# MoE block on one core: the order of the experts ends with each group's smallest one, and most output rows are summed and stored during the last weight loads

## The chip, the cores and the metric

The kernel runs on one core of a Trainium2 chip. The metric is the device time of one execution in microseconds (us), lower is better; three runs of the kernel before took 1245.50, 1245.51 and 1246.52 us, median 1245.51 us.

## The reference

One layer: a layer norm, a token mixer (gMLP and gated DeltaNet), a second layer norm `h1`, a hierarchical mixture of experts, a third layer norm. There are 512 tokens of width 1024. Only the mixture and the last norm matter here:

```python
grp = argmax(softmax(xt @ w_rg + b_rg))           # one of 4 groups for each token
le = (xt @ w_re + b_re)[token, grp]               # 8 experts in that group
top_v, top_i = lax.top_k(le, 2)                   # the token's two experts
gate = p_grp * softmax(top_v)
y_e = (silu(x @ w1[e]) * (x @ w3[e])) @ w2[e]     # for each of its two experts
out = layer_norm(alpha * h1 + gate_1 * y_1 + gate_2 * y_2, ln2_g, ln2_b)
```

All 32 experts are stored; an expert that gets no token need not be computed. Both experts of a token lie in the same group. Routing the reference's own inputs gives these numbers of tokens, expert 0 first, a row for each group: 1 0 2 2 1 2 1 1; 57 55 40 18 94 83 37 130; 34 22 82 104 15 18 126 19; 0 11 8 5 26 15 13 2. Two experts (1 and 24) are empty. No expert has over 160 tokens.

## The kernel before, in words

Up to about 700 us the mixer, `h1` and the router run. The router (`Router`) turns the choice of each token into `ord`, the order in which experts are worked on, and into lists of token indices for each place in that order. `Router.order` (L1088) sees only the first 256 tokens, since it has to be ready before the rest are routed.

The experts are then streamed (`Experts.run`, L1313). A "block" b is a place in the order, 0 to 31. Each block has six weight loads of 1 MB: chunks 0 to 3 are w1 and w3, chunks 4 and 5 are w2. SyncE (SP) issues them (`load_big`, L391) into a ring of 18 buffers (`raws`), in the order (b, 0 to 3), (b-1, 4), (b-1, 5). A load waits until the tensor engine (PE) has read what lay in its buffer, and until the load eight back has landed, because there are eight semaphores for SP's and ScalarE's transfers. From block 3 on a block without tokens skips its loads.

In iteration b the PE does `up` for block b (L1440), transposes the next block's tokens (`turn_x`, L1407), does `down` for block b-1 (L1467) and transposes the hidden values of block b (`turn`, L1457). ScalarE (ACT) and VectorE (DVE) form silu and product in `gate` (L1450). A block of n tokens is done in a small part of 32 rows and up to two large parts of 64, whichever its count needs (`units`, L1247). At the end of an iteration `store_y` (L1478) copies the outputs of block b-1 out of PSUM and GpSimd (POOL) issues five conditional stores to `y_dram`. POOL also gathers the tokens of block b+2 (`fetch`).

In the order before, experts go round the groups, the ones that look empty are put together ahead of the last four, and the last four are simply the last non-empty ones. For these inputs the blocks 24 and 25 are empty and the last four blocks have 126, 13, 130 and 19 tokens.

After the last block comes everything else: `finish_rows` (L1004) loads h1 (four tiles of 128 tokens by 1024) and the rows of the norms' gains and biases, 4.2 MB, and forms alpha * (h1 * g + b). A loop over blocks of overflowing experts (L1661) runs zero times here, but all engines meet there with all their transfers done. `finish` (L1022) gathers eight tiles of 128 rows of `y_dram` (L1028), adds them with their gates to the four tiles (L1034), takes the statistics (L362 to L374), normalizes (ACT, L1037), applies gain and bias (L1038, L1039) and stores the four tiles (L1040).

Of the kernel before, what the change touches and what calls it, by code (L numbers as in the profile page):

```python
# [1043 lines left out]
class Router:  # L1044
# [43 lines left out]
    def order(self):  # L1088
# [9 lines left out]
        v.tensor_scalar(f.rearrange("p (j g) -> p j g", g=4), self.cps[:, NT].rearrange("p (g j) -> p j g", g=4),
                        0.0, None, op0=OP.is_gt)
        v.memset(f[:, 0:NPRE], 1.0)  # L1100
        r = W.tile([128, E], F32, name="or_")
        v.tensor_tensor_scan(r, cst["ones"][:, 0:E], f, 0.0, OP.mult, OP.add)
# [7 lines left out]
        v.scalar_tensor_tensor(out=p1, in0=r, scalar=-1.0, in1=p1, op0=OP.add, op1=OP.add)  # L1110
        v.tensor_tensor(out=p1, in0=p1, in1=p0, op=OP.subtract)
        v.tensor_tensor(out=p1, in0=p1, in1=f, op=OP.mult)
        v.tensor_tensor(out=p0, in0=p0, in1=p1, op=OP.add)
        eq = W.tile([128, E, E], F32, name="oeq")
# [621 lines left out]
```

## Time and profile before

| what | us |
|---|---|
| median of three runs | 1245.51 |
| the profiled execution: its own time | 1246.53 |
| its span, first to last instruction | 1244.8 |
| last matmul ends | 1187.3 |
| eight gathers start | 1200.2 |
| last DVE instruction ends | 1239.1 |

Busy in the span: PE 1039.3 us, DVE 646.2, ACT 403.1, POOL 193.5. The table of 40 slices is read like this: each digit is the busy share of 31.1 us in tenths. The transfers are at 9 in nearly all slices from the 24th to the 37th, and in the last three, after the last weights, no engine and no queue is at 9.

In the timeline rows the first number is the start in us, the second the duration; "x4" is the number of instructions merged in the row; in brackets stand the engine's idle time before it and what ended that. In rows of windows the columns are: stretch, its length, busy time (and count) of PE, its weight loads, DVE, ACT, POOL, the granted PE clock, the busy share of the 16 DMA engines, GB/s.

### The profile page before, as it was taken

The numbers are of one execution on the slowest core, as the hardware profiler recorded it, in microseconds if no ns is written. First come the engines' busy times: TensorE is split into PE (matmuls) and PEld (weight loads), VectorE is DVE, ScalarE is ACT, GpSimd is POOL, SyncE is SP. The second block draws the span as 40 slices with busy tenths as digits, with TensorE's granted clock in tenths as the row PEclk, the third lists the DMA queues.
The fourth block names the chain that finished last, engine by engine and source line by source line (L and its number), as shares of the span: only waits on it lengthen the run. The fifth ranks groups of instructions, "written<-read, shape, count | busy, mean of one in ns | idle before, by whom it ended". The sixth has DMA issues, their size and how long they took to land. (4 is left out here: it accounts for less than half of the span.)

```text
span 1244.8 us, 19415 instructions
## 1 busy us (share of the span) xinstructions
PE 1039.3 (83%) x6880; PEld 687.0 (55%) x6880; DVE 646.2 (52%) x1356; ACT 403.1 (32%) x844; POOL 193.5 (16%) x377
## 2 busy tenths in 40 slices
PE   4999999999999999999999588787877586579810
PEld 2888788867777777667887333443333242234300
DVE  7566444567667777754865444533223232433246
ACT  6333355444555455435431311111111111211111
POOL 1000100212212132200001101111111101111043
PEclk9999999999999999999999698997979897799965
DMA  5422533899221121114672799999999999999832
GB/s 172 153 84 69 160 95 110 284 341 362 70 68 58 45 68 52 34 52 152 238 308 91 295 385 409 391 411 400 414 390 415 399 414 399 377 387 387 349 115 111
DMA packets 76899, 296.10 MB, mean 238 GB/s; under 512 B 9328, under 2 KB 34176, under 8 KB 53216
## 3 DMA queue, kind: packets, MB, share of 16 engines
q1 hardware_dynamic: 66672, 272.13, 58.0%
q0 software_dynamic: 7504, 17.20, 4.3%
q10 hardware_dynamic: 2592, 4.99, 1.2%
q8 instruction: 87, 1.43, 0.5%
q14 instruction: 44, 0.36, 0.1%
HBM read 277.36 MB, written 50.35 MB: 263 GB/s over the span
## 5 line engine op out<-in xcount | busy, mean ns | idle before, releaser
L214 PE MATMUL psi<-hTh,lo 128*128 128x512 f32 x448 | 183.0, 410 | 1.6 <-DVE lo L214 1.6
L214 PE MATMUL psi<-hTh,hi 128*128 128x512 f32 x448 | 183.5, 413 | 0.9 <-ACT hi L214 0.5
L214 PE MATMUL psi<-hTl,hi 128*128 128x512 f32 x448 | 183.1, 411 | 0.0
L1455 DVE TENSOR_TENSOR h<-h,u 128x640 f32<-128x640 f32 x32 | 26.3, 822 | 279.2 <-ACT h L1454 267.2
L214 DVE TENSOR_TENSOR lo<-raw,hi 128x1024 fp32r<-128x1024 f32 x74 | 91.3, 1234 | 79.6 <-ACT hi L214 78.9
L1447 PE MATMUL u<-raw,xs 128*32 128x256 f32 x1472 | 102.1, 426 | 29.8 <-DMA raw<-in_w 28.2
L214 ACT CAST hi<-raw 128x1024 fp32r<-128x1024 f32 x74 | 77.5, 1047 | 117.3 <-PE psi L214 100.2
L1447 PE MATMUL u<-raw,x 128*64 128x512 f32 x448 | 103.6, 618 | 5.9 <-PEq L1387 2.9
L214 PEld LDWEIGHTS psi<-hTh,lo 128*128 128x128 f32 x448 | 84.4, 188 | 21.3 <-issue 3.9
L214 PEld LDWEIGHTS psi<-hTh,hi 128*128 128x128 f32 x448 | 84.6, 189 | 20.3 <-issue 2.8
L214 PEld LDWEIGHTS psi<-hTl,hi 128*128 128x128 f32 x448 | 84.4, 189 | 17.2 <-issue 1.6
L1447 PEld LDWEIGHTS u<-raw,xs 128*32 128x32 f32 x1472 | 50.9, 120 | 73.4 <-DMA raw<-in_w 38.6
L1454 ACT ACTIVATE h<-u 128x640 f32<-128x640 f32 x32 | 22.6, 705 | 204.5 <-PEq L1389 160.9
L1447 PEld LDWEIGHTS u<-raw,x 128*64 128x64 f32 x448 | 35.5, 143 | 68.6 <-issue 60.0
L1475 PE MATMUL y<-raw,hT 128*64 128x512 f32 x224 | 60.1, 672 | 11.5 <-PEq L1387 9.2
L1475 PE MATMUL yz<-raw,hT 128*32 128x256 f32 x736 | 55.2, 437 | 16.4 <-PEq L1427 5.9
L1464 ACT COPY hT<-t 128x128 f32<-128x128 f32 x32 | 8.5, 266 | 184.0 <-PE t L1461 172.7
L1483 DVE COPY ysmall<-yz 32x256 f32<-32x256 f32 x128 | 53.3, 417 | 16.8 <-PE yz L1475 15.3
L214 DVE SCALAR_TENSOR_TENSOR acc<-xp,cols,acc 128x512 f32<-128x512 f32 x72 | 54.7, 760 | 4.7 <-ACT acc L214 3.5
L1492 POOL DMA_DIRECT2D y_dram<-ylarge x128 | 19.5, 155 | 194.1 <-DMA y_dram<-ysmall 114.8
L1475 PEld LDWEIGHTS yz<-raw,hT 128*32 128x32 f32 x736 | 26.3, 121 | 35.7 <-issue 18.0
L1422 PE MATMUL t<-ident,mh 64*128 64x64 f32 x256 | 23.5, 237 | 25.8 <-PEq L1389 20.0
(437 smaller groups left out, 1864.9 us busy)
## 6 DMA issues: line engine op xcount, KB each, us to landing
raw<-in_w SPq DMA_DIRECT2D x192, 1024.0 KB
raw<-in_wt SPq DMA_DIRECT2D x73, 512.0 KB
y_dram<-zero SPq DMA_DIRECT2D x48, 512.0 KB
y_dram<-ylarge POOLq DMA_DIRECT2D x128, 128.0 KB
raw<-in_wv SPq DMA_DIRECT2D x8, 512.0 KB
raw<-in_wo SPq DMA_DIRECT2D x4, 1024.0 KB
y_dram<-ysmall POOLq DMA_DIRECT2D x32, 128.0 KB
vt<-in_x SPq DMA_DIRECT2D x4, 512.0 KB
```

The lines of the kernel that those rows point to most:

```text
L214: op._ins = getattr(getattr(self.nc, op.attr), op.name)(*map(real, op.args), **{k: real(x) for k, x in op.kw.items()})
L1422: nc.tensor.transpose(self.t[0][:, k * NA:k * NA + NA], r[0][:, k * 128:k * 128 + 128], ident[0:NA, 0:NA])
L1447: self.nc.tensor.matmul(self.u[q * r:(q + 1) * r, NP if p is None else p, 0:c], x[:, k, r0:r0 + r], self.raw[b, k // 2][:, o:o + c], start ...
L1454: self.nc.scalar.activation(out=h, in_=u[:, :, 0], func=AF.Silu)
L1455: self.nc.vector.tensor_mul(out=h, in0=h, in1=u[:, :, 1])
L1464: self.nc.scalar.copy(out=x[:, n], in_=self.t[1][:, 0:128])
L1475: self.nc.tensor.matmul(y[q * r:(q + 1) * r, 0:c], t[:, i, j * r:(j + 1) * r], self.raw[b, 4 + k // 2][:, o:o + c], start=k == 0, stop=k == 3)
L1483: nc.vector.tensor_copy(out=small[:, q], in_=self.y0[q * 32:(q + 1) * 32, 0:256])
L1492: nc.gpsimd.dma_start(out=dst[:, q * 512:(q + 1) * 512], in_=large[q * 64:(q + 1) * 64, p], cond=n > 32 + 64 * p)
```

## The change

It has five parts.

1. **Order of the experts.** The groups still take turns, but each expert that looks empty is moved back by 10.5 places among the others, and the expert of each group with the fewest (at least one) of the first 256 tokens goes to the last four places. For these inputs the empty experts stand at blocks 10 and 12 (and two experts that only look empty, with 1 and 2 tokens, at 26 and 27), the blocks 22 and 24 have 126 and 130 tokens, and the last six blocks 1, 2, 2, 18, 5 and 15. Since both experts of a token are of one group, a token is in the last four blocks at most once.
2. **Loads.** From block RT = 26 on, the chunks of block b go into the buffers of block b-2. The six buffers of block 23 are thereby free for other use, and the ring is 12 buffers deep from then on. The last two chunks of block 25 are loaded ahead of the first four of block 26.
3. **The other rows.** A new class `Tail` is called at the head and the end of each iteration from 26 on. It loads the rows of gains and biases and h1 (iteration 26, now issued by ACT), gathers for the tokens' rows outside the last four blocks (29 and 30; rows of the last four blocks point to a row of zeros), adds, normalizes and stores all four tiles (30 and 31).
4. **The late rows.** The tokens of the last four blocks, up to 32 each, have a tile `F` of their own: 4 x 32 rows with their h1, their gates and their other expert's output. The outputs of the last four blocks stay in a buffer `Y` and are not stored to `y_dram`. The last block's part is added from PSUM, then comes the norm of `F`, and a scatter writes its rows over the ones stored before; it waits for the four stores.
5. **The branch.** `flag` is zero if each of the last four blocks has at most 32 tokens, no two non-empty ones are of a group, and nothing overflows. If it isn't, the whole of the old finish runs after all, ahead of the last step. For these inputs (2, 18, 5 and 15 tokens, four groups) it is zero.

The diff, cut to its core:

```diff
@@ Router.order
+        f = W.tile([128, E], F32, name="of_")
+        v.tensor_scalar(f, self.cps[:, NT], 0.0, None, op0=OP.is_gt)
+        v.scalar_tensor_tensor(out=sc, in0=self.cps[:, NT], scalar=32.0, in1=cst["jx"], op0=OP.mult, op1=OP.add)
...
+        v.tensor_reduce(out=mn, in_=gj(sc), axis=AX.X, op=OP.min)
+        v.tensor_tensor(out=gj(lt), in0=gj(sc), in1=bc(mn, 8, 2), op=OP.is_equal)
...
+        v.scalar_tensor_tensor(out=f, in0=f, scalar=-10.5, in1=cst["seq"], op0=OP.mult, op1=OP.add)
+        v.scalar_tensor_tensor(out=f, in0=lt, scalar=128.0, in1=f, op0=OP.mult, op1=OP.add)
+        eq = W.tile([128, E, E], BF, name="oeq")
+        v.tensor_tensor(out=eq, in0=bc(f, E, 1), in1=bc(f, E, 2), op=OP.is_lt)
+        v.tensor_reduce(out=pos, in_=eq, axis=AX.X, op=OP.add)
+        v.tensor_tensor(out=eq, in0=bc(pos, E, 1), in1=bc(cst["iota"][:, 0:E], E, 2), op=OP.is_equal)
@@ Experts.run
+            if tail and b == RT:
+                steps = steps[:-6] + steps[-2:] + steps[-6:-2]
-                self.raw[b, c] = kk.load_big(blk[1]()[c], conds.get(b))
+                self.raw[b, c] = kk.load_big(blk[1]()[c], conds.get(b), self.raw[b - 2, c] if b >= RT else None)
...
+            if tail and b >= RT:
+                tail(b, 0)
             if b < nb:
                 self.parts(b, self.up)
-                load(4)
+                if not tail or b not in (RT - 3, E - 2):
+                    load(4)
@@ class Tail, __call__
+        if (b, at) == (RT, 0):
...
+            self.load_rows(R_L1G, R_L1B)
+            for x in (self.g2, self.b2):
+                act.activation(out=x, in_=x, func=AF.Copy, scale=ALPHA)
+            for t in range(NT):
+                act.dma_start(out=self.f[t], in_=self.h1_dram[t * 128:(t + 1) * 128, :])
...
+        elif (b, at) == (RT + 3, 0):
+            self.take(0, 1)
+        elif (b, at) == (RT + 4, 0):
+            self.add(0, 1)
+            self.take(2, 3)
+            self.gather(self.O, self.y_dram, r.lrow, NYROW)
+        elif (b, at) == (RT + 4, 1):
+            self.apply((0, 1), self.stats(0, 1))
+        elif (b, at) == (RT + 5, 0):
+            self.add(2, 3)
+            v.scalar_tensor_tensor(out=self.F, in0=self.O, scalar=r.lgate[:, 1:2], in1=self.F, op0=OP.mult, op1=OP.add)
+            self.m = self.stats(2, 3)
+        elif (b, at) == (RT + 5, 1):
+            self.apply((2, 3), self.m)
...
+        elif (b, at) == (E, 2):
+            for q in range(4):
+                f = F[128 - 32:128, q * 256:(q + 1) * 256]
+                v.scalar_tensor_tensor(out=f, in0=ex.y0[q * 32:(q + 1) * 32, 0:256], scalar=r.lgate[128 - 32:128, 0:1], in1=f,
+                                       op0=OP.mult, op1=OP.add)
...
+            x = g.indirect_dma_start(out=kk.a["out"], out_offset=bass.IndirectOffsetOnAxis(ap=r.lidx, axis=0), in_=F,
+                                     in_offset=None, bounds_check=T - 1, oob_is_err=False)
@@ build
-    kk.finish_rows(h1_dram)
...
+    flag = nc.values_load(r.flag[0:1, 0:1], min_val=0, max_val=64, skip_runtime_bounds_check_because="sums of counts")
+    with tc.If(flag > 0):
...
+        kk.finish_rows(h1_dram)
...
+        kk.finish(RS, r, y_dram)
+        nc.vector.tensor_scalar(r.lidx, r.ordl, 0.0, float(T), op0=OP.mult, op1=OP.add)
+    with tc.manual_schedule():
+        tail(E, 2)
```

What is left out: `Router.rest` forms the late rows' indices, gates, `flag` and the gather's indices with some 30 small DVE instructions spread over the first iterations, and a 12 KB table in memory; a second constant `jx`.

On SP, the end of its queue before (in_w2 is w2 of the last two blocks; the h1 and row loads of `finish_rows` follow):

```order
L399 DMA raw9_5390<-in_w2 128x2048
L399 ISA
L399 DMA raw10_5391<-in_w2 128x2048
L1387 UNCONDITIONAL_BRANCH
L1389 UNCONDITIONAL_BRANCH
L399 ISA
L399 DMA raw11_5392<-in_w2 128x2048
L1013 DMA raw12_5393<-h1_dram_57 128x1024 x2
L1387 UNCONDITIONAL_BRANCH
L1389 UNCONDITIONAL_BRANCH
L1013 DMA raw13_5394<-h1_dram_57 128x1024 x2
L1015 DMA raw14_5395<-in_rows 128x1024 x2
```

And with the change, the same place:

```order
L402 DMA raw9_5396<-in_w2 128x2048
L402 ISA
L402 DMA raw14_5401<-in_w2 128x2048
L1456 UNCONDITIONAL_BRANCH
L1458 UNCONDITIONAL_BRANCH
L402 ISA
L402 DMA raw15_5402<-in_w2 128x2048
L1456 UNCONDITIONAL_BRANCH
L1458 UNCONDITIONAL_BRANCH
L1688 DMA out<-raw11_5398 128x1024 x2
L1857 TENSOR_LOAD flag_5442
L1858 COMPARE_AND_BRANCH
```

The h1 and row loads have left SP's queue; two of the four output stores stand behind the last weight load, and then comes the branch on `flag`.

On POOL, the gathers of `y_dram` before (`yi` holds the row of each token's output; the stores are those of the last block, the branch is the loop over overflowing blocks):

```order
L1492 DMA y_dram_59<-ylarge_11918 64x512
L1661 REGISTER_ALU
L1661 COMPARE_AND_BRANCH
L1661 UNCONDITIONAL_BRANCH
L1028 DMA raw16_5397<-y_dram_59,yi_5429 128x1024 x2
L1028 DMA raw17_5398<-y_dram_59,yi_5429 128x1024 x2
L1028 DMA raw4_4806<-y_dram_59,yi_5429 128x1024 x2
L1028 DMA raw5_4807<-y_dram_59,yi_5429 128x1024 x2
```

With the change, iteration 30 on POOL (`yie` are the rows with the late ones replaced, `lrow` the other rows of the late tokens, `mh` the buffer O):

```order
L1658 DMA raw12_5399<-y_dram_59,yie_5436 128x1024 x2
L1658 DMA raw13_5400<-y_dram_59,yie_5436 128x1024 x2
L1456 UNCONDITIONAL_BRANCH
L1458 UNCONDITIONAL_BRANCH
L1658 DMA mh_4466<-y_dram_59,lrow_5441 128x1024
L1496 UNCONDITIONAL_BRANCH
L1500 UNCONDITIONAL_BRANCH
L1456 UNCONDITIONAL_BRANCH
L1458 UNCONDITIONAL_BRANCH
L1567 ISA
L1567 DMA y_dram_59<-ylarge_11554 64x512
```

The gathers now stand between iterations of the expert loop, ahead of the conditional stores of a block that has no large part, and no longer behind the loop's branch.

On DVE, from the product in `gate` of the last block (`h`) to the branch, before (the copies take the two last blocks out of PSUM; L1019 and L1020 form h1 * g + b):

```order
L1455 TENSOR_TENSOR h_11532<-h_11532,u_5407 128x640
L1387 UNCONDITIONAL_BRANCH
L1389 UNCONDITIONAL_BRANCH
L1483 COPY ysmall_11578<-yz_5406 32x256 x4
L1387 UNCONDITIONAL_BRANCH
L1389 UNCONDITIONAL_BRANCH
L1483 COPY ysmall_11632<-yz_5406 32x256 x4
L1019 TENSOR_TENSOR raw12_5393<-raw12_5393,raw14_5395 128x1024 x2
L1020 TENSOR_TENSOR raw12_5393<-raw12_5393,raw14_5395 128x1024
L1659 TENSOR_LOAD nov_5426
L1661 COMPARE_AND_BRANCH
```

And with the change (the copies go to `Y`, L1685 and L1687 are gain and bias of tiles 2 and 3, the 96x1024 instruction adds the first three late blocks to `F`):

```order
L1524 TENSOR_TENSOR h_11692<-h_11692,u_5413 128x640
L1456 UNCONDITIONAL_BRANCH
L1458 UNCONDITIONAL_BRANCH
L1557 COPY raw7_4812<-yz_5412 32x256 x4
L1685 TENSOR_TENSOR raw11_5398<-raw11_5398,raw6_4811 128x1024 x2
L1456 UNCONDITIONAL_BRANCH
L1458 UNCONDITIONAL_BRANCH
L1687 TENSOR_TENSOR raw11_5398<-raw11_5398,raw6_4811 128x1024
L1629 SCALAR_TENSOR_TENSOR raw7_4812<-raw7_4812,lgate_5440 96x1024
L1857 TENSOR_LOAD flag_5442
L1858 COMPARE_AND_BRANCH
```

Tiles 2 and 3 get their gain and bias between the last block's `gate` and the branch, on the same queue; the last block's copies are gone from there.

More of the change, by code (lines that the diff above doesn't have):

```diff
@@ L1039, in finish, with behind @@
             (nc.gpsimd if t < 3 else v).tensor_tensor(out=f, in0=f, in1=self.l2b, op=OP.add)
-            nc.sync.dma_start(out=a["out"][t * 128:(t + 1) * 128, :], in_=f)
+            self.behind(nc.sync.dma_start(out=a["out"][t * 128:(t + 1) * 128, :], in_=f), self.stores)
+    def behind(self, x, others):
+        for y in others:
+            self.tc.add_manual_dep(x.ins, y.ins.name, mybir.DependencyInfo(
+                mybir.DependencyClass.Sync, mybir.DependencyReason.DATA), reason="rows of the output")
 class Router:
@@ L1096, in order @@
                 nc.tensor.matmul(self.cps[:, NT], cst["ones_bf"], q[:, k], start=t + k == 0, stop=t + k == 2)
+        gj = lambda x: x.rearrange("p (g j) -> p g j", g=4)
         f = W.tile([128, E], F32, name="of_")
[L1098 to L1102, printed above, removed]
@@ L1110, in order @@
[L1110 to L1114, printed above, removed]
-        v.tensor_tensor(out=eq, in0=bc(p0, E, 1), in1=bc(cst["iota"][:, 0:E], E, 2), op=OP.is_equal)
-        g.tensor_tensor(out=eq, in0=eq, in1=bc(cst["seq"], E, 1), op=OP.mult)
+        v.tensor_scalar(f, self.cps[:, NT], 0.0, None, op0=OP.is_gt)
@@ L1194, in rest @@
         v.tensor_copy(out=self.nov, in_=inc[:, NX * E - 1:])
+        v.tensor_tensor(out=fs[:, 0:1], in0=fs[:, 0:1], in1=inc[:, NX * E - 1:], op=OP.add)
+        v.tensor_copy(out=self.flag, in_=fs[:, 0:1])
         exc = R.tile([128, NX, E], F32, name="exc")
@@ L1311, in clear, with run @@
                                       func=AF.Copy, scale=0.0)
-    def run(self, blocks, more=None, clear=None):
+    def run(self, blocks, more=None, clear=None, tail=None):
         nc, kk, nb = self.nc, self.kk, len(blocks)
@@ L1367, in run @@
                 self.parts(b - 1, self.down)
-                load(2)
+                if not tail or b != RT - 2:
+                    load(2)
             next(more, None)
@@ L1371, in run @@
                 self.turn(b)
-            if b:
-                self.store_y(b - 1)
+            if b and not (tail and b == nb):
+                self.store_y(b - 1, tail)
             next(more, None)
+            if tail and b >= RT:
+                tail(b, 1)
     def n(self, b, e=ET.PE, i=0):
@@ L1476, in down, with late, store_y @@
                                       self.raw[b, 4 + k // 2][:, o:o + c], start=k == 0, stop=k == 3)
-    def store_y(self, b):
+    def late(self, i):
+        return self.Y[32 * i:32 * i + 32].rearrange("r (q n) -> r q n", q=4)
+    def store_y(self, b, tail=None):
         nc, row = self.nc, self.blocks[b][0]
-        small = self.yp.tile([32, 4, 256], F32, name="ysmall")
+        i = b - (E - NL)
+        late = tail and i >= 0
+        small = self.late(i) if late else self.yp.tile([32, 4, 256], F32, name="ysmall")
         large = self.yp.tile([128, NP, 512], F32, name="ylarge")
@@ L1485, in store_y @@
             nc.scalar.copy(out=large[:, p], in_=self.y[p])
-        n, d, r0 = (self.n(b, ET.Pool, i) for i in range(3))
-        nc.gpsimd.dma_start(out=self.y_dram[ds(row + r0, 32), :], in_=small.rearrange("r q n -> r (q n)"), cond=d > 0)
+        n = self.n(b, ET.Pool)
+        if not late:
+            self.store_small(b, small)
         for p in range(NP):
```

178 lines of the change are left out of this document (159 added, 19 removed).

## The prediction

> **What bounds the kernel now.** I read the table of slices first (the transfers are at 9 from the 24th slice on), then the stretches of the second half by windows:
>
> ```profile
> 722.00:1050.00 328.00, 254.74 (x2370) 118.97 (x2368) 121.00 (x250) 55.41 (x110) 46.60 (x131) 0.89 1.01 404
> 1050.00:1060.00 10.00, 8.44 (x56) 3.25 (x52) 1.58 (x3) 1.23 (x3) 1.50 (x6) 1.00 0.95 383
> 1060.00:1070.00 10.00, 4.21 (x37) 2.05 (x30) 5.74 (x12) 2.53 (x5) 1.07 (x6) 0.78 0.78 296
> 1070.00:1177.00 107.00, 83.88 (x722) 39.85 (x722) 34.43 (x68) 17.74 (x35) 14.15 (x43) 0.91 1.01 398
> 1177.00:1187.40 10.40, 10.34 (x73) 3.80 (x69) 1.67 (x4) 1.83 (x4) 1.04 (x2) 0.94 0.14 42
> 1187.40:1202.00 14.60, 0.00 (x0) 0.00 (x0) 7.08 (x9) 2.97 (x4) 4.07 (x9) 0.65 0.21 48
> 1202.00:1218.00 16.00, 0.00 (x0) 0.00 (x0) 12.19 (x13) 0.00 (x0) 10.09 (x8) 0.50 0.80 262
> 1218.00:1244.80 26.80, 0.00 (x0) 0.00 (x0) 16.68 (x25) 4.96 (x4) 11.16 (x7) 0.50 0.20 79
> ```
>
> The last two columns say it: from 722 to 1177 us the transfers set the pace (share 1.01, about 404 GB/s) but for a hole at 1050 to 1070; after 1177 us nothing is full, and 68 us pass in steps that wait for each other. The timeline shows where the weights end, and the PE:
>
> ```profile
> 1149.44 13.95 PE L1447 MATMUL u<-raw,x 128*64 128x512 f32 x64
> 1162.32 7.83 SPq L1015 DMA_DIRECT2D raw<-in_rows  x4
> 1167.58 3.66 PE L1447 MATMUL u<-raw,xs 128*32 128x256 f32 x64
> 1177.15 7.59 PE L1475 MATMUL y<-raw,hT 128*64 128x512 f32 x32
> 1185.40 1.93 PE L1475 MATMUL yz<-raw,hT 128*32 128x256 f32 x32
> ```
>
> ```profile
> SPq L1015 <- DMA raw<-in_w: 8.4, 4, 2.1
> ```
>
> Each of the four row loads waited for a weight load; the last was issued at 1162.32 + 7.83 - 0.33 = 1169.8 us, when the last weights had been seen to land. h1 and the rows, 4.2 MB or 10.4 us at 404 GB/s, were moved behind the weights until 1177, so the weights' data ended near 1166.6 and were seen 3 us later. The PE is behind by then: block 30 has two large parts (the 13.95 and 7.59 us), and it ends at 1187.3. The chain of waits then goes on alone:
>
> ```profile
> 1187.54 10.02 DMA y_dram<-ylarge
> 1197.57 0.09 POOLq L1661
> 1200.18 0.35 POOL raw L1028
> 1204.80 6.04 DMA raw<-y_dram,yi
> 1237.83 1.23 DVE raw L1039
> ```
>
> Stores 10 us, the loop's meeting of engines 2.6 us, gathers 11, arithmetic to 1239.1, last store to 1244.8.
>
> **The change, part by part.** The sum goes in time of the profiled execution.
>
> *Transfers up to the last weight.* The change moves work under the weights, but there the transfers are full, so its bytes are paid in full. (a) The hole goes: two empty blocks in a row let the queue run dry; at blocks 10 and 12 one block with loads stands between them. The hole is 10 x (1.01 - 0.95) + 10 x (1.01 - 0.78) = 2.9 us; -2.9. (b) h1 and rows are moved ahead of the last weight; the 1177 already holds them; 0. (c) The eight gathers of 0.5 MB: their stretch was busy 16 x 0.80 = 12.8 us; +12.8. (d) The ninth (O), an eighth of that; +1.6. (e) Stores of tiles 0 and 1: the last stretch holds four stores, 26.8 x 0.20 = 5.4 us; half; +2.7. (f) Four small stores of 128 KB go, and four of block 30's large stores, after 1177 before, come under the weights; 0.131 MB at 404 GB/s is 0.3 us each, so they cancel. Data of the last weight end at 1177 - 2.9 + 12.8 + 1.6 + 2.7 = 1191.2, seen at 1194.
>
> *Last block.* The PE has half of a small `down` left, 1.93 / 2 = 1.0: 1195. But tiles 2 and 3 stand ahead on DVE:
>
> ```profile
> 1163.44 0.70 ACT L1454 ACTIVATE h<-u 128x640 f32<-128x640 f32 x1 [15.92 <-PE u L1447]
> 1164.18 0.82 DVE L1455 TENSOR_TENSOR h<-h,u 128x640 f32<-128x640 f32 x1 [21.96 <-ACT h L1454]
> 1185.47 0.59 ACT L1465 COPY hT<-t 128x512 f32<-128x512 f32 x1
> 1185.95 1.08 ACT L1485 COPY ylarge<-y 128x512 f32<-128x512 f32 x2
> ```
>
> ```profile
> L1034 DVE SCALAR_TENSOR_TENSOR raw<-raw,g,raw 128x1024 f32<-128x1024 f32 x8 | 10.0, 1269 | 3.8 <-DMA raw<-y_dram,yi 3.8
> L1039 POOL TENSOR_TENSOR raw<-raw,raw 128x1024 f32<-128x1024 f32 x3 | 8.1, 2687 | 4.1 <-DVE raw L1038 3.2 <-DVE nm L374 0.9
> L1038 DVE TENSOR_TENSOR raw<-raw,raw 128x1024 f32<-128x1024 f32 x4 | 5.8, 1445 | 1.6 <-ACT raw L1037 1.6
> L362 DVE BATCH_NORM_STATS2 st<-raw 128x6 f32<-128x512 f32 x8 | 5.4, 683 | 0.0
> L1037 ACT ACTIVATE raw<-raw,nm,rs 128x1024 f32<-128x1024 f32 x4 | 5.0, 1239 | 35.9 <-DVE nm L374 35.9
> L1483 DVE COPY ysmall<-yz 32x256 f32<-32x256 f32 x4 | 1.7, 418 | 8.5 <-PE yz L1475 8.4
> L368 DVE BATCH_NORM_AGGREGATE mv<-st 128x2 f32<-128x12 f32 x4 | 0.8, 204 | 0.1
> L370 DVE TENSOR_SCALAR ve<-mv 128x1 f32<-128x1 f32 x4 | 0.6, 151 | 0.1
> ```
>
> The `up` of block 31 can start four loads before the end: 1194 - 4 x 2.6 (1.05 MB at 404 GB/s) = 1183.6. Then `up` 3.7, silu 0.7, product 0.8, `down` of block 30 1.9 beside them, transposes about 1, ACT's copies 0.3 + 0.6 + 1.1, tiles 2 and 3 on ACT 2 x 1.24, and DVE behind the second: gain 1.2, bias 1.2, late rows 1.3. Laid end to end, with the PE's `down` ending about 1190, the late add ends at 1199. The read of `flag` and the jump I price like the loop's before, 1197.57 to 1200.18, 2.6 us; below, 0 if it hides. So the last step starts at 1195 by PE and at 1201.7 by DVE; I take 1201, near the DVE's end, since every term of it has a row.
>
> *Last step.* Four additions from PSUM, priced like the copies, 4 x 0.42, statistics 2 x 0.68, 0.20, 0.15, two passes 2 x 1.27 (POOL's power lies beside the first): 5.9 us, 1206.9. The scatter from SBUF isn't in the trace. Bounds: the last store took from 1239.1 to 1244.8, 5.7; a first gather 5.6, and POOL's issue of 1 to 2 us comes on top:
>
> ```profile
> 1200.18 2.07 POOL L1028 DMA_INDIRECT raw<-y_dram,yi  x1 [5.57 <-issue]
> 1205.77 1.28 DVE L1034 SCALAR_TENSOR_TENSOR raw<-raw,g,raw 128x1024 f32<-128x1024 f32 x1
> 1207.02 0.99 POOL L1028 DMA_INDIRECT raw<-y_dram,yi  x1 [0.30 <-issue]
> ```
>
> I take 5.7 + 1.0 = 6.7, between 5.6 and 7.8. The span ends at 1213.6. The execution's own time was 1246.53 for a span of 1244.8, 1.7 more, and the median 1.0 below that execution: 1213.6 + 1.7 - 1.0 = 1214.3. **Forecast 1214 us**, 2.5% less.
>
> *A rule that speaks against it.* Of the gathers before, the one at 1200.18 lay beside a DVE instruction and took 2.07 us on POOL, the one at 1207.02 beside none 0.99: 1.1 us more. The Trainium skill, page SBUF — State Buffer, section "SBUF: two separate sides", says of transfers issued from GpSimd that a DVE instruction which holds the shared port pair keeps their descriptors from being written until it is over. The trace agrees in sign. In the change all nine gathers stand in iterations with DVE's additions; at the row's 1.1 us each the five of iteration 30 come 5.4 us later. The sum takes this as covered by the some 15 us to the next iteration; uncovered it is a rival.
>
> *Router.* `order` gains a comparison and a sum over 128x1024:
>
> ```profile
> 667.13 1.22 DVE L1115 TENSOR_TENSOR oeq<-op,iota 128x1024 f32<-128x1024 f32 x1
> 670.93 1.22 DVE L1117 TENSOR_REDUCE ord<-oeq 128x32 f32<-128x1024 f32 x1 [2.57 <-POOL oeq L1116]
> 672.78 0.18 PE L1127 MATMUL cps<-M,ustrict 128*128 128x32 bf16 x1 [0.67 <-DVE M L1125]
> 695.11 0.19 PE L1127 MATMUL cps<-M,ustrict 128*128 128x32 bf16 x1 [2.70 <-DVE M L1125]
> ```
>
> That is 2.4 us more until `ord` is known. The PE waited 0.67 us for it, and has products of the next tile to do instead; the lists end with the last tile, at 695, which `order` doesn't set. 0, at most +2.4 if that cover is gone. The small DVE additions of `rest` lie where DVE is busy 121 of 328 us and the transfers bound: 0. ACT waits for rows and older loads in iteration 26, with `gate` of block 26 behind it; two tokens' work, covered by loads ahead.
>
> **The rivals.**
>
> 1. *The shorter ring starves the loads.* Blocks 22 and 24 (126 and 130 tokens) follow closely, and the load of block 26 waits for block 24's `up`. For block 22, the small block 23 and the `up` of 24 the PE needs (13.95 + 7.59) + (3.66 + 1.93) + (13.95 + 3.66) = 45 us, with two to three us a block between them (from 1163.4 to 1167.6, where `up` gives way to `up`, 4 us hold 1.9 of products) some 52, against two blocks of loads, 12 x 2.6 = 31, so it ends 21 us behind; ten loads, 26 us, are queued there. For it: the granted clock was 0.78 to 1.00, and at 0.8 the 52 become 60. Against: 5 us of slack. Price 3 to 10 us: 1217 to 1224.
> 2. *The last chain is longer*: gathers beside DVE (5.4 us, by the two rows above), POOL's additions of 2.7 us ahead of its small powers, or engines fetching code behind the branch. 1219 to 1227.
> 3. *The chain is hidden*: PE, not DVE, ends last: 1195 + 5.9 + 5.7 = 1206.6, a time of 1207.
> 4. *The change doesn't do what it says, and is slower*: `flag` isn't zero. Then the old finish follows: 1195 + 57.5 (1187.3 to 1244.8) + some 10 us of loads and products no longer under the weights + the last step of 12.6 = 1275, a time near 1276. It decides from one of the last four blocks having over 32 tokens, or two of a group. Against: 2, 18, 5, 15 of four groups; the 13.95 us of block 30 before fit the same counts (130).
>
> **How the numbers follow.** Forecast 0.66, rival 1 0.10, rival 2 0.12, rival 3 0.07, rival 4 0.03, else (a stall that eats all) 0.02. The range takes the forecast, rivals 1 and 2 and the upper part of 3's way: 1205 to 1227. About 0.2% (2.5 us) can be told from no change here; all but rival 4 and half of the rest lie far below: faster 0.94, same 0.02, slower 0.04.
>
> **What would show it.** Right: a transfer share of 1.0 through 1060 and up to about 1190; gathers and output stores before the last weights; DVE's late add after the PE's last matmul; one scatter at the end, some 13 us after that. Wrong: a share under 0.9 near blocks 25 to 27 (rival 1); over 15 us from last matmul to end with idle engines (2); the overflow loop or the eight gathers of the old finish running at all (4). The prediction is wrong if the end lies outside the range or the gathers come after the weights.

## The result and the profile after

The changed kernel is slower: median 1261.24 us of four runs (1258.14 to 1263.45) against 1245.51 of the kernel before; ratio 1.0127, 95% interval 1.0097 to 1.0157. The forecast was 1214. The profiled execution took 1258.14 us for a span of 1256.4, and since the forecast's sum was made in spans, 1213.6 stands against 1256.4: 42.8 us.

The stretches by windows (columns as before) show what became of the weights:

```profile
860.00:870.00 10.00, 10.00 (x50) 4.01 (x48) 0.00 (x0) 0.00 (x0) 1.12 (x6) 1.00 0.79 301
1080.00:1090.00 10.00, 10.00 (x83) 4.07 (x77) 3.59 (x8) 0.99 (x3) 1.68 (x6) 1.00 0.65 250
1090.00:1100.00 10.00, 1.96 (x40) 0.91 (x28) 0.00 (x0) 2.95 (x4) 5.90 (x8) 0.78 0.88 284
1150.00:1200.00 50.00, 27.25 (x262) 11.79 (x254) 16.11 (x26) 5.07 (x10) 10.28 (x18) 0.64 1.02 413
1200.00:1238.50 38.50, 4.95 (x37) 2.51 (x37) 27.23 (x32) 7.16 (x9) 12.69 (x17) 0.54 0.17 69
1238.50:1256.40 17.90, 0.00 (x0) 0.00 (x0) 6.06 (x10) 0.00 (x0) 2.58 (x2) 0.50 0.06 23
```

The hole of before moved to 860 and a second one came at 1080: 10 x (1.01 - 0.79) + 10 x (1.01 - 0.65) + 10 x (1.01 - 0.88) = 7.1 us instead of 2.9. From 1100 to 1200 the transfers are full, then 56 us follow with nothing full. GpSimd's timeline says why:

```profile
1161.27 0.99 POOL L1658 DMA_INDIRECT raw<-y_dram,yie  x1 [0.30 <-issue]
1179.18 0.04 POOL L1567 DMA_DIRECT2D y_dram<-ylarge  x1 [16.91 <-DMA raw<-y_dram,yie]
1186.70 0.99 POOL L1658 DMA_INDIRECT mh<-y_dram,lrow  x1 [0.30 <-issue]
1203.66 0.04 POOL L1567 DMA_DIRECT2D y_dram<-ylarge  x1 [15.97 <-DMA mh<-y_dram,lrow]
1205.07 0.58 POOL L375 TENSOR_TENSOR rse<-vee,mhalf 128x1 f32<-128x1 f32 x1
```

The rows of 0.04 us are `store_y`'s conditional stores of large parts; the condition is false, nothing is moved. But a store to `y_dram` waits for the gathers that read `y_dram`, in brackets 16.91 and 15.97 us, and behind the second of them in the queue stands the power of tile 0 (GpSimd's part of the norm, `rse`). VectorE and the PE wait in turn:

```profile
1187.09 0.15 DVE L373 TENSOR_SCALAR vee<-mve 128x1 f32<-128x1 f32 x1
1205.68 0.16 DVE L377 SCALAR_TENSOR_TENSOR nme<-mve,rse 128x1 f32<-128x1 f32 x1 [18.44 <-POOL rse L375]
1212.87 7.07 DVE L1674 SCALAR_TENSOR_TENSOR raw<-raw,g,raw 128x1024 f32<-128x1024 f32 x4
1226.08 0.82 DVE L1524 TENSOR_TENSOR h<-h,u 128x640 f32<-128x640 f32 x1
1238.55 2.00 DVE L1635 SCALAR_TENSOR_TENSOR raw<-yz,lgate,raw 32x256 f32<-32x256 f32 x4 [0.66 <-DMA out<-raw]
```

```profile
1194.92 1.93 PE L1544 MATMUL yz<-raw,hT 128*32 128x256 f32 x16 [2.60 <-DMA raw<-in_w]
1226.95 0.48 PE L1530 MATMUL t<-ident,h 128*128 128x128 f32 x1 [30.10 <-DVE h L1524]
1228.76 3.62 PE L1544 MATMUL yz<-raw,hT 128*32 128x256 f32 x32 [0.47 <-issue]
```

The last wait for weights ends at 1194.92. Then the PE stands 30.1 us for the product of block 31 (L1524), which is in VectorE's queue behind tiles 0 to 3. The last step starts at 1238.55, its scatter is issued at 1245.51, and the span ends 10.9 us later.

### The profile page after: what moved, and what is told of

It is laid out like the page before. It is cut to its first block, busy times and chain, and to the rows that moved or that the text cites. A ratio compares the mean times of both kernels' runs of the same rounds, so it can differ in the third digit from the quotient of the medians.

```text
span 1256.4 us, 19381 instructions
## 1 busy us (share of the span) xinstructions
PE 1041.6 (83%) x6880; PEld 689.3 (55%) x6880; DVE 662.6 (53%) x1401; ACT 401.9 (32%) x842; POOL 208.7 (17%) x384
## 5 line engine op out<-in xcount | busy, mean ns | idle before, releaser
L1524 DVE TENSOR_TENSOR h<-h,u 128x640 f32<-128x640 f32 x32 | 26.3, 821 | 243.3 <-ACT h L1523 237.6
L216 DVE TENSOR_TENSOR lo<-raw,hi 128x1024 fp32r<-128x1024 f32 x74 | 91.4, 1236 | 81.6 <-ACT hi L216 80.5
L1516 PE MATMUL u<-raw,xs 128*32 128x256 f32 x1472 | 98.7, 417 | 33.7 <-DMA raw<-in_w 32.1
L1544 PE MATMUL yz<-raw,hT 128*32 128x256 f32 x736 | 65.5, 504 | 18.6 <-DMA raw<-in_w 7.4
L1544 PE MATMUL y<-raw,hT 128*64 128x512 f32 x224 | 54.7, 630 | 7.8 <-PEq L1456 7.6
L1544 PEld LDWEIGHTS yz<-raw,hT 128*32 128x32 f32 x736 | 29.5, 138 | 43.9 <-issue 25.5
L1557 DVE COPY ysmall<-yz 32x256 f32<-32x256 f32 x112 | 46.7, 417 | 6.3 <-PE yz L1544 5.2
```

Of the source, the lines that this page charges most:

```text
L216: op._ins = getattr(getattr(self.nc, op.attr), op.name)(*map(real, op.args), **{k: real(x) for k, x in op.kw.items()})
L1516: self.nc.tensor.matmul(self.u[q * r:(q + 1) * r, NP if p is None else p, 0:c], x[:, k, r0:r0 + r], self.raw[b, k // 2][:, o:o + c], start ...
L1524: self.nc.vector.tensor_mul(out=h, in0=h, in1=u[:, :, 1])
L1544: self.nc.tensor.matmul(y[q * r:(q + 1) * r, 0:c], t[:, i, j * r:(j + 1) * r], self.raw[b, 4 + k // 2][:, o:o + c], start=k == 0, stop=k == 3)
L1557: nc.vector.tensor_copy(out=small[:, q], in_=self.y0[q * 32:(q + 1) * 32, 0:256])
```

## The experiments

Theories: **1**, GpSimd's queue (skipped stores that wait for gathers, with the powers behind them); **2**, VectorE's order (the gate of block 31 behind the additions); **3**, gathers and weights share the transfers and that sets the end. Theories 5 and 6, on the hole at 1080 and on the first stage, came later (there is no 4). Each ratio is to runs of the kernel before on the same chip. The medians of those runs lie between 1243.60 and 1245.51 us, so a difference between medians from two chips can be off by some 2 us.

| run | median, us | ratio (95% interval) | last step starts | span ends |
|---|---|---|---|---|
| changed kernel | 1261.24 | 1.0127 (1.0097 to 1.0157) | 1238.55 | 1256.4 |
| e1_no_late_large | 1240.77 | 0.9970 (0.9952 to 0.9989) | 1221.41 | 1239.3 |
| e2_gate_first | 1254.95 | 1.0092 (1.0058 to 1.0126) | 1233.15 | 1251.0 |
| e3_both | 1242.93 | 0.9983 (0.9964 to 1.0001) | 1224.22 | 1242.1 |
| e4_order_only | 1241.93 | 0.9974 (0.9957 to 0.9990) | | 1238.7 |
| e5_rows_pool | 1257.80 | 1.0102 (1.0068 to 1.0135) | 1237.36 | 1255.9 |
| e6_half_loads | 1243.93 | 0.9995 (0.9972 to 1.0017) | 1228.33 | 1246.2 |
| e7_plain_store | 1237.92 | 0.9938 (0.9917 to 0.9959) | 1219.82 | 1234.9 |
| e9_pipelined_once | 1238.59 | 0.9949 (0.9932 to 0.9966) | 1219.87 | 1237.7 |
| e10_rows_sync | 1239.67 | 0.9970 (0.9951 to 0.9989) | 1218.29 | 1236.1 |
| e11_no_pool_end | 1233.01 | 0.9922 (0.9903 to 0.9941) | 1220.12 | 1230.3 |
| e12_vector_only | 1230.31 | 0.9888 (0.9868 to 0.9908) | 1211.29 | 1229.1 |
| e13_jx_alone | 1249.10 | 1.0036 (1.0017 to 1.0055) | | 1249.1 |
| e14_order_jx_late | 1238.32 | 0.9953 (0.9935 to 0.9972) | | 1236.1 |
| e15_after_jx_late | 1256.66 | 1.0104 (1.0070 to 1.0138) | 1232.80 | 1250.7 |
| e16_vector_only_jx_late | 1227.91 | 0.9873 (0.9841 to 0.9904) | 1206.03 | 1223.9 |

**e1, the skipped stores left out.**

```diff
@@ store_y
-        for p in range(NP):
+        for p in range(0 if late else NP):
```

> Leaves out the conditional stores of the large parts of blocks 28 to 30 (these inputs never carry one of them out; another input could need them). Theory 1 (POOL's queue: those stores, though skipped, wait for the gathers to land, and the powers of tiles 0 and 1 stand behind them, so DVE waits 18 us for them with the gate of block 31 behind): the powers come at about 1188, the gate of block 31 at about 1209 instead of 1226, time 1244, 17 us less than the changed kernel. Rival 2 (the gathers' landing and DVE's order alone set the gate): DVE would wait as long for the rows themselves, 0 to 5 us less, 1256 to 1261.

Theory 1 was right: 20.5 us between the medians (17 expected), the last step 17.1 us earlier. The power of tile 0 in e1, now waiting for VectorE's own statistics only, and VectorE's timeline:

```profile
1187.94 0.58 POOL L375 TENSOR_TENSOR rse<-vee,mhalf 128x1 f32<-128x1 f32 x1 [4.49 <-DVE vee L373]
```

```profile
1192.47 3.35 DVE L1685 TENSOR_TENSOR raw<-raw,raw 128x1024 f32<-128x1024 f32 x1 [0.16 <-ACT raw L1683]
1195.74 7.07 DVE L1674 SCALAR_TENSOR_TENSOR raw<-raw,g,raw 128x1024 f32<-128x1024 f32 x4
1208.96 0.82 DVE L1524 TENSOR_TENSOR h<-h,u 128x640 f32<-128x640 f32 x1
1221.41 2.00 DVE L1635 SCALAR_TENSOR_TENSOR raw<-yz,lgate,raw 32x256 f32<-32x256 f32 x4 [0.66 <-DMA out<-raw]
```

The gate comes at 1208.96, as expected. VectorE now hardly waits; it works. Twelve skipped instructions of 0.04 us each cost 1.6% of the kernel.

**e2, the gate ahead of the additions; e3, both edits.**

```diff
@@ Tail.__call__
-        elif (b, at) == (RT + 5, 0):
+        elif (b, at) == (RT + 5, 1):
             self.add(2, 3)
...
-        elif (b, at) == (RT + 5, 1):
             self.apply((2, 3), self.m)
```

> The additions of tiles 2 and 3, the ninth gather's addition and the statistics of tiles 2 and 3 stand behind the gate, the turn and the stored block of iteration 31 instead of ahead of them. Theory 1 (POOL's queue holds DVE until 1205.7 in any case): the gate of block 31 comes at about 1209, but DVE has the same 20 us of work behind it, so the last step starts near 1230 instead of 1238.5: 8 us less, 1253. Rival 2 (DVE's order is the cause, POOL's wait would lie beside it): the gate comes at 1191, the end falls by 15 us or more, 1246 or less.

> Both edits of the two runs before (leaves out the same stores that these inputs don't carry out). Theories 1 and 2 together: gate of block 31 at 1191 to 1195, additions of tiles 2 and 3 as their rows land (1193 to 1203), last step from 1216, span 1234, time 1238, 23 us less than the changed kernel and 7 less than the kernel before. Rival 3 (the rows land late because gathers share the transfers with the weights, and that alone sets the end): no better than the better of the two single edits.

e2 fell by 6.3 us, near theory 1's value (8), not theory 2's (15), and its gate of block 31 came at 1211.85 (theory 1: 1209): the waiting stores are still there. In e3 the gate of block 31 came at 1198.29, and it brought nothing over e1. The profile of e3 shows the same mistake in another place:

```profile
1198.29 0.82 DVE L1524 TENSOR_TENSOR h<-h,u 128x640 f32<-128x640 f32 x1
1203.78 1.73 DVE L1557 COPY raw<-yz 32x256 f32<-32x256 f32 x4 [4.67 <-PE yz L1544]
1205.54 5.12 DVE L1673 SCALAR_TENSOR_TENSOR raw<-raw,g,raw 128x1024 f32<-128x1024 f32 x4
```

The additions now stand behind the copy of block 30's output, which waits for the last weights, and the 20 us of VectorE's work from there to the last step come after it. Rival 3's number came out (no better than e1); its reason fell in e10, where the weights came 6.5 us earlier and the end hardly moved.

**e4, the order alone.** The kernel before with the new `order` (and its constants).

> The kernel before with the new order of blocks and nothing else of the change. If the order brings what I took it for: the last block has few tokens, the PE ends some 8 to 13 us earlier behind the weights, and the known finish of 57 us follows: 1233 to 1237. If the order itself costs (the two holes in the transfers at 860 and 1080 to 1100 belong to it): the holes show in this run too and the gain falls to 5 or less, 1240 to 1246.

Only 3 us came (ratio 0.9974). There is no hole at 1080 to 1100 (share 1.01 and 1.02), so that hole isn't the order's. The PE ended at 1175.5, 11.8 us earlier than before, but the gathers started only 6.5 us earlier, at 1193.72: each block's large stores, though skipped, are reached 4.65 to 5.74 us behind its small one, in waits that the profile puts down to stores to `y_dram`, and the last two short blocks come closely one behind the other. Where the rest went came out in e13.

**e5, rows and h1 issued by GpSimd; e10, by SyncE** (e10 on the basis of e9, below).

```diff
@@ Tail
-                act.dma_start(out=self.f[t], in_=self.h1_dram[t * 128:(t + 1) * 128, :])
+                g.dma_start(out=self.f[t], in_=self.h1_dram[t * 128:(t + 1) * 128, :])
...
-            self.nc.scalar.dma_start(out=x, in_=row_bc(self.kk.a["rows"], row))
+            self.nc.gpsimd.dma_start(out=x, in_=row_bc(self.kk.a["rows"], row))
```

> The changed kernel with the loads of the rows and of h1 (iterations 26 and 28) issued from GpSimd instead of ScalarE; nothing else. Theory 5 (the hole in the transfers at 1080 to 1100 comes from SyncE's weight load waiting for the semaphore that it shares with ScalarE's row load, which ScalarE issues only after its copies for block 24): the shares of 0.65 and 0.88 go to 1.0, weights end 4 to 5 us earlier, time 1256. Rival (the ring of two blocks starves the loads, as my first rival had it, or the order): the hole stays, time 1261 plus or minus 1.

The hole at 1080 goes. In the changed kernel ScalarE issues the row loads only at 1089.54, behind its copies for block 24, and among what SyncE waits for from 1060 to 1120 are the transfers of that queue (second row, 12.1 us). With GpSimd as issuer a new hole opens at 1180, because the tokens' gathers for the next blocks came late. Changed kernel, then e5 by windows and by what the PE waits for:

```profile
1089.54 0.34 ACTq L1655 DMA_DIRECT2D raw<-in_rows  x1
...
SPq L402 <- DMA raw<-h_dram: 12.1, 4, 3.5
```

```profile
1080.00:1090.00 10.00, 9.55 (x73) 3.87 (x73) 4.55 (x9) 0.50 (x1) 1.21 (x6) 1.00 1.01 418
1090.00:1100.00 10.00, 6.94 (x111) 4.17 (x109) 0.00 (x0) 1.83 (x4) 3.62 (x6) 0.99 1.01 416
1185.00:1190.00 5.00, 2.06 (x21) 0.70 (x13) 4.50 (x7) 0.00 (x0) 1.06 (x5) 0.50 0.43 141
```

```profile
PE t L1491 <- DMA mh<-h_dram,idx: 27.8, 3, 12.8
```

> As e9_pipelined_once, with the loads of rows and h1 issued from SyncE between its own weight loads instead of from ScalarE. In e5 GpSimd issued them: the hole at 1080 to 1100 went, but GpSimd's row gathers for the next blocks came late and a hole of some 7 us opened at 1180 to 1190. Theory 5: with SyncE neither is there, weights end 4 to 5 us earlier and the end follows, 4 us below e9. Rival (VectorE's work and not the weights sets the end by then): 0 to 1 us below e9.

In e10 neither hole at 1080 nor at 1185 is there and the PE reads its last weights of block 30 by 1194.2, 6.5 us earlier than in e9. Those products in e9, then in e10:

```profile
1198.76 1.94 PE L1546 MATMUL yz<-raw,hT 128*32 128x256 f32 x16 [1.71 <-DMA raw<-in_w]
```

```profile
1190.51 3.64 PE L1546 MATMUL yz<-raw,hT 128*32 128x256 f32 x32 [6.42 <-ACT h L1525]
```

The last step starts only 1.6 us earlier and the time is not better (1239.67 after 1238.59, the intervals overlap). By then the weights no longer set the end; the rival had it.

**e6, weight loads in halves.**

```diff
@@ load_big (blocks 28 to 31)
-            self.nc.sync.dma_start(out=raw, in_=src, cond=cond)
+            for i in range(2):
+                q = slice(i * 1024, i * 1024 + 1024)
+                self.nc.sync.dma_start(out=raw[:, q], in_=src[:, q], cond=cond)
```

> As e1_no_late_large, with the weight loads of blocks 28 to 31 issued as two halves, so that a row of a transfer is 4 KB like a gather's and not 8 KB. In e1 the four gathers of tiles 0 and 1 land some 3.6 to 4.6 us apart under the weights, 0.52 MB or a third of the 415 GB/s. If the transfers take turns row by row between the two queues, the gathers now get half: 2.5 us apart, the addition of tile 1 ends near 1176 instead of 1181. If a gather is slow by itself (its descriptors, its queue), they stay 4 us apart. The bytes are the same, so the weights end as late and the time moves by 0 to 5 us, 1236 to 1241.

VectorE's additions of tiles 0 and 1 follow the landings. The first two in e1 and in e6:

```profile
1167.63 1.28 DVE L1674 SCALAR_TENSOR_TENSOR raw<-raw,g,raw 128x1024 f32<-128x1024 f32 x1 [7.41 <-DMA raw<-y_dram,yie]
1171.42 1.28 DVE L1674 SCALAR_TENSOR_TENSOR raw<-raw,g,raw 128x1024 f32<-128x1024 f32 x1 [2.50 <-DMA raw<-y_dram,yie]
```

```profile
1168.84 1.28 DVE L1679 SCALAR_TENSOR_TENSOR raw<-raw,g,raw 128x1024 f32<-128x1024 f32 x1 [4.94 <-DMA raw<-y_dram,yie]
1171.39 1.28 DVE L1679 SCALAR_TENSOR_TENSOR raw<-raw,g,raw 128x1024 f32<-128x1024 f32 x1 [1.26 <-DMA raw<-y_dram,yie]
```

3.6 to 4.6 us apart became 2.55: a gather of 0.52 MB got about a third of 415 GB/s beside loads of 8 KB rows and half beside 4 KB rows. The Trainium skill, page DMA: Bandwidth & Descriptors, section Queues, rings and completion order, says that a transfer engine takes turns between queues packet by packet; the two spacings agree if a packet is a row. The time did not fall (1243.93, expected 1236 to 1241): VectorE was done with tile 1 at 1177.8 instead of 1180.9, but then stood 5.13 us for the silu of block 30 and 4.93 us for the product whose output it copies next. The PE had read its last weights by 1206.4, in e1 by 1201.0; why they came later isn't shown, and the profiled execution of e6 lies 3.9 us above its median.

**e7, a plain store for the scatter; e11, also no power on GpSimd at the end.**

```diff
@@ Tail.__call__, (E, 2)
-            x = g.indirect_dma_start(out=kk.a["out"], ...)
+            x = nc.sync.dma_start(out=kk.a["out"][0:128, :], in_=F)
```

> As e1_no_late_large, with the last indirect store of the 128 late rows replaced by a plain store of the same 0.5 MB from SyncE to the first 128 rows of the output (so it leaves out the scattering of the rows). In e1 the end came 10.9 us after the last addition's end (1228.1 to 1239.3), and GpSimd's last instruction waited some 7 us of it after the data had landed. If the indirect store from GpSimd is what that wait belongs to, the end comes 5.7 us after the last addition, as with the last store of the kernel before: 5 us less, 1235.5. If the end of the program costs this in any case, 1240 as e1.

> As e7_plain_store, with the last step's power left out as well (a copy on VectorE in its place), so that GpSimd's last instruction is the addition of tile 2, some 9 us before the last addition on VectorE. In e7 GpSimd's closing instruction still ended 8.9 us after GpSimd's last work (the power), in the kernel before 8.8 us after its last addition, in e1 9.0 us after the indirect store. If the program ends some 8.8 us after GpSimd's last work whatever that is, the plain store now ends last: the span ends 4 to 4.5 us after VectorE's last addition (8.4 in e7), time 1233 to 1234, 4 us less than e7. If this wait belongs to the end of the program itself, it stays at 8.4: 1237.

e7's span ended 8.4 us after the last addition, not 5.7. GpSimd's closing instruction is the longest of its three rows DRAIN at the program's end. These rows in the kernel before, the changed kernel, e7 and e11 (duration in ns least, middle, most; first and last start):

```profile
L1732 POOLq DRAIN  x3: 46/104/11427, 1232.6 to 1244.6; - x3
```

```profile
L1940 POOLq DRAIN  x3: 46/110/10298, 1245.3 to 1256.1; - x3
```

```profile
L1939 POOLq DRAIN  x3: 46/110/10474, 1223.6 to 1234.6; - x3
```

```profile
L1939 POOLq DRAIN  x3: 46/101/8887, 1220.1 to 1230.0; - x3
```

The long one starts beside GpSimd's last work and ends a fixed time behind it: before, 1235.24 to 1244.0, 8.8 us; changed kernel, from the scatter's issue (1246.57) 9.0; e1 9.0; e4 8.8; e7, from the power (1225.16) 8.9. So even the kernel before ended with it and not with its last store, which had landed at 1241.7. In e11, where GpSimd's last work is the end of the branch, at 1220.07, it took 8.9 us and ended at 1229.0, beside the store's landing at 1229.4; the span ended 3.7 us after the last addition. Between e7 and e11 the spans differ by 4.6 us and the medians by 4.9, but the ratios, whose intervals overlap, only by 2.0: the rows show what ended each span, the runs don't show the gain in time clear of noise.

**e8 and e9, one tile at a time, late stores to a tensor of their own.**

```diff
@@ store_y
+            if late:
+                dst = self.y2_dram[i * NB + 64 * p:i * NB + 64 * p + 64, :]
@@ Tail.__call__ (3: a call behind gate and turn_x of the iteration)
+        elif (b, at) == (RT + 4, 3):
+            self.add(0)
+            self.take(2)
+            m = self.stats(0)
+            self.add(1)
+            self.take(3)
+            self.gather(self.O, self.y_dram, r.lrow, NYROW)
+            self.m = m + self.stats(1)
...
+        elif (b, at) == (RT + 5, 0):
+            self.add(2)
+            self.m = self.stats(2)
+        elif (b, at) == (RT + 5, 3):
+            self.add(3)
...
@@ build, if flag > 0
+        nc.gpsimd.dma_start(out=y_dram[(E - NL) * NB:E * NB, :], in_=y2_dram)
```

> Keeps the whole computation. The large parts of the last four blocks go to a tensor of their own (copied over in the branch), so that their skipped stores wait for no gather; the additions and statistics of tiles 0 to 3 are issued one tile at a time behind the gate of their iteration (tile 2 ahead of the gate of 31). Theories 1 and 2 together (GpSimd's queue and VectorE's order, with some 30 us of VectorE's work left behind 1195 in e1): VectorE works on tile 0 while tile 1's gathers land, the last step starts some 8 to 12 us earlier than e1's 1221: time 1229 to 1233. Rival 3 (gathers and weights share the transfers and that sets the end, as e3 suggests, where the weights ended 8 us later): no better than e1, 1238 to 1243.

> What e8_pipelined was meant to be: that kernel ran the last step twice (its new call in the loop had the number by which the last step is called, so in iteration 32 too), here it has a number of its own. The whole computation. Theories 1 and 2: no skipped store waits for a gather, each gate stands ahead of the additions behind it, VectorE works on tile 0 while tile 1's gathers land; the last step starts at 1208 to 1212 instead of e1's 1221, time 1228 to 1234. Rival 3 (the transfers set the end): no better than e1, 1238 to 1243.

e8 gave 1251.21 with its last step run twice and tells nothing. e9 fell short of theories 1 and 2: the last step started at 1219.87, 1.5 us before e1's. With GpSimd's additions beside it, VectorE's own rows are long. In e10, GpSimd and VectorE:

```profile
1191.75 3.26 POOL L1698 TENSOR_TENSOR raw<-raw,raw 128x1024 f32<-128x1024 f32 x1 [2.91 <-DVE raw L1696]
1195.94 2.36 POOL L1698 TENSOR_TENSOR raw<-raw,raw 128x1024 f32<-128x1024 f32 x1
```

```profile
1192.72 6.68 DVE L1685 SCALAR_TENSOR_TENSOR raw<-raw,g,raw 128x1024 f32<-128x1024 f32 x2
1202.76 2.60 DVE L1685 SCALAR_TENSOR_TENSOR raw<-raw,g,raw 128x1024 f32<-128x1024 f32 x2
```

Two additions take 6.68 us beside GpSimd's and 2.60 alone. Gathers suffer too: in e9 the two that were issued in the middle of VectorE's additions took 1.92 and 1.96 us on GpSimd, the other seven 0.99 to 1.01. An addition and the gather beside it, in e9:

```profile
1177.79 2.60 DVE L1685 SCALAR_TENSOR_TENSOR raw<-raw,g,raw 128x1024 f32<-128x1024 f32 x2
```

```profile
1179.34 1.92 POOL L1669 DMA_INDIRECT raw<-y_dram,yie  x1 [15.37 <-DVE raw L1685]
```

**e12, halves, and all bias additions on VectorE.**

```diff
@@ Tail.apply
-            (nc.vector if t == 3 else nc.gpsimd).tensor_tensor(out=self.f[t], in0=self.f[t], in1=self.b2, op=OP.add)
+            nc.vector.tensor_tensor(out=self.f[t], in0=self.f[t], in1=self.b2, op=OP.add)
```

> As e10_rows_sync (the whole computation), with two further edits that its trace points to. The weight loads of blocks 28 to 31 go as two halves, as in e6, so that gathers land 2.55 us apart instead of 3.8: VectorE ends tile 1's additions some 5 us earlier. The additions of the bias of tiles 0 to 2 are VectorE's instead of GpSimd's: in e10 VectorE's two additions of tile 2 took 3.3 us each where GpSimd's bias lay beside them and 1.28 elsewhere, and the gain of tile 3's bias 3.25 instead of 1.2, so 6 us of VectorE's time go and 3.7 of its own come. If VectorE's work is what sets the end, the last step starts 4 to 7 us earlier than e10's 1218.3, time 1233 to 1236. If the transfers or GpSimd do, it stays at 1238 to 1240. By VectorE's own durations alone, without the loss beside GpSimd, the bias costs 3 us: 1242.

The last step starts 7.0 us earlier, the time is 1230.31. The run has both edits at once, but the traces part them: VectorE comes to the copy of block 30's output 3.9 us earlier (1184.82, in e10 1188.69), and from there to the last step, where the biases lie, it takes 26.5 us instead of 29.6. In that stretch VectorE has three bias additions more and is done 3.1 us sooner; rows of e12:

```profile
1188.84 2.35 DVE L1703 TENSOR_TENSOR raw<-raw,raw 128x1024 f32<-128x1024 f32 x2
1191.11 2.60 DVE L1690 SCALAR_TENSOR_TENSOR raw<-raw,g,raw 128x1024 f32<-128x1024 f32 x2
1211.29 2.00 DVE L1651 SCALAR_TENSOR_TENSOR raw<-yz,lgate,raw 32x256 f32<-32x256 f32 x4 [0.36 <-DVEq L1876]
```

**e13 to e16, one constant.** Comparing traces from the start showed that all kernels with the new order so far begin their experts at 708 to 712 us instead of 704.8, and lose 5 to 6 us by 36 us of the first stage. What they add there is the constant `jx`.

```diff
@@ consts
-        iota("jx", [128, E], [[0, 4], [1, 8]], 0, 0)
@@ build, ahead of the router
+    nc.gpsimd.iota(c["jx"], pattern=[[0, 4], [1, 8]], base=0, channel_multiplier=0, ...)
```

> The kernel before plus one unused instruction: the 0.25 us GpSimd instruction that makes the changed kernel's new constant (jx, 128x32) among the first constants. Theory 6 (that constant shifts the list order in which the recorded first stage is issued: ScalarE's cast of weights that have not landed stands ahead of the activation that the PE waits for, and the PE stands 6 us at 30 to 36 us): the first stage is 5 to 6 us longer and all that follows comes as much later, 1249 to 1251, 5 us slower than before. Rival (the changed kernels' first stage is later for another reason, or the loss is made up before the experts start): 1244 to 1246.

> As e4_order_only (the kernel before with the new order), with the constant made behind the recorded stage, just ahead of the router. Theory 6: the first stage is as in the kernel before, e4's 1241.9 falls by 5 to 6 us, 1236 to 1237: the order itself is worth 8 us, as I took it for. Rival (no loss in the first stage): 1241 to 1242.

> The changed kernel with the constant made behind the recorded stage and nothing else. Theory 6: 1255 to 1256, 5 to 6 us below the changed kernel, and the expert stage starts at 703 to 705 as before instead of at 708 to 710. Rival: 1260 to 1262.

> As e12_vector_only (the whole computation), with the constant made behind the recorded stage. Theory 6: 1230.3 falls to 1224 to 1226, 1.5% below the kernel before. Rival: 1230.

e13, the kernel before plus one unused instruction of 0.25 us, is slower by 4.1 us (ratio 1.0036, 1.0017 to 1.0055). ScalarE and the PE in the kernel before, then in e13:

```profile
28.60 1.51 ACT L214 ACTIVATE f<-psi,cols 128x128 f32<-128x128 f32 x4 [0.27 <-PE psi L214]
...
30.81 0.79 PE L214 MATMUL pv<-yah,hTh 128*128 128x512 f32 x1 [2.25 <-ACT hTh L214]
```

```profile
33.10 1.04 ACT L214 CAST hi<-raw 128x1024 fp32r<-128x1024 f32 x1 [4.33 <-DMA raw<-in_wv]
34.05 1.50 ACT L214 ACTIVATE f<-psi,cols 128x128 f32<-128x128 f32 x4
...
36.25 0.80 PE L214 MATMUL pv<-yah,hTh 128*128 128x512 f32 x1 [6.17 <-ACT hTh L214]
```

The layer that records the first stage and issues it as a list puts the instructions in another order when one is added: now a cast that waits 4.33 us for weights stands ahead of the activation that the PE needs, and the PE stands 6.17 us. Without it e14 fell by 3.6 us from e4, e15 by 4.6 from the changed kernel, e16 by 2.4 from e12 (by the ratios 2.6, 2.9 and 1.9). The sign is shown by e13 alone beyond doubt; in the pairs the intervals overlap, and the sizes are below the 5 to 6 that I expected. In e16 the experts start at 703.1 instead of e12's 710.0 and the span ends 5.2 us earlier. e16 has the whole computation and is the fastest: ratio 0.9873 (0.9841 to 0.9904) to the kernel before.

## Why the prediction was wrong

The sum missed the span's end by 42.8 us: the last step started 37.5 us late (1238.55 for 1201), it took 7.0 us instead of 5.9, and from the scatter's issue to the end 10.9 instead of 6.7.

- *Hole goes, -2.9*: wrong, 7.1 us of holes instead of none. One moved with the empty blocks, the other came from the row loads on ScalarE, which I had priced at "0 ... covered by loads ahead". It did not decide: the last weights were seen at 1194.92, forecast 1194. That agreement is luck. The holes made it 7.1 us later than the sum, and the experts began 3.4 us later (708.13 for 704.78); but the stores of tiles 0 and 1, which the sum put under the weights (2.7), came after them, and so did gathers, with the transfers full until about 1202, some 7 us.
- *Last block*: **the step that failed.** "I take 1201" for the start of the last step laid VectorE's work behind the weights as if tiles 0 and 1 were done and tiles 2 and 3 added; it came at 1238.55. I priced the large stores that come under the weights by their bytes (0.3 us each), and put at nothing what a *skipped* one waits for (16.91 and 15.97 us) and holds up behind it on GpSimd. That is 17.1 of the 37.5 us (e1). A further 10.1 (e1's 1221.41 to e12's 1211.29) went in steps of 1.5 (e9, VectorE's order), 1.6 (e10, the holes) and 7.0 (e12, the landing of gathers and VectorE's loss beside GpSimd). 5.3 (e12 to e16) go with the first stage in the profiled executions; the medians show 2.4 of them. 5.0 are left between e16's 1206.03 and 1201: there VectorE works from the gate of block 31 (1191.08) to the last step almost without a stop, on additions, statistics, gain and bias of tiles 2 and 3, and of that the sum had only 3.7 us (gain, bias, late rows). That this accounts for all of the 5.0 is argued, not shown.
- *Gathers, 12.8 + 1.6*: as bytes right, but landing one in 4 us beside the weights and not in 1.6, which moves tile 0 and all behind it; the prediction priced the bytes and not the landing.
- *Last step, 5.9*: 7.0; the power was not wholly hidden (0.44 us), and additions and the step to the scatter's issue took a little more.
- *Scatter, 6.7*: 10.9. My row, the last store of the kernel before to its end, was misread: GpSimd's closing instruction ended that span. Its 8.8 to 9.0 us behind GpSimd's last work now start at the scatter.
- *Router, 0*: wrong by a route that I hadn't looked at. The instructions in `order` cost nothing that can be seen (with the constant moved, e14's experts begin at 704.79, before at 704.78); the constant cost 4 us in a stage 600 us earlier.
- *The rule weighed*: the 1.1 us per gather did not come in the changed kernel, but it wasn't tried there either. Its nine gathers took 0.98 to 1.01 us on GpSimd beside VectorE's copies, statistics and small products; none lay beside an addition of 128x1024. Where two gathers each did, in e9 and e12, it came: 1.91 to 1.97 us. The Trainium skill, page SBUF — State Buffer, section "SBUF: two separate sides", also describes a lock on the port pair that VectorE and GpSimd share: whichever instruction starts first has it for its whole length. e10's rows above, for additions on both, agree.
- *Rivals*: rival 1 had the place (1080 to 1100) and the size (4.9, in its 3 to 10) but not the cause: SyncE waited for the PE only 1.0 us from 1060 to 1120. Rival 2 had the cause's neighbourhood (GpSimd's additions ahead of its small powers) and 5 to 13 us for it; the end came 42.8 us late. Rival 4 didn't happen. The chance of slower, 0.04, rested on the branch and on an unnamed stall; no rival said that an engine in order may hold all others up for a transfer that isn't made.

## What to carry to other kernels

Walk the in-order queue of every engine past each step that is moved, skipped instructions included: a conditional store that isn't made still waits for all that it would have to. Before calling work "hidden under the weights", add up the one engine that does it (VectorE in e1 was still busy for 27.8 us after 1195) and ask how late its data land when two queues share the transfers. And compare the traces from their first microsecond: with an issue order made by a list or a planner, one instruction more can take away much of what its change brings (here 4.1 us in e13, where the new order brings 6.7 in e14).

## What the runs showed of the hardware that I had not expected

- GpSimd's closing instruction ended 8.8 to 9.0 us after GpSimd's last work in each of seven kernels, whether that was an addition, a power, an indirect store or the branch's end; a program whose last work is GpSimd's pays all of it.
- Transfers of two queues shared by rows: a gather of 0.52 MB in 4 KB rows took 3.6 to 4.6 us beside 8 KB rows, about a third of the rate, and 2.55 us beside 4 KB rows, half of it.
- VectorE's additions of 128x1024 took 1.3 us alone and 3.3 beside an addition on GpSimd, and GpSimd's 2.3 became 3.3: in e12 the three bias additions were cheaper on the busier engine, by 3.1 us. Gathers issued from GpSimd in the middle of such an addition took 1.9 to 2.0 us instead of 1.0.
